# Order of the scatter products in three pairs of experts, the engine of every fifth low part, and the count of filler products

## The chip, the cores and the metric

The kernel runs on one core of one Trainium2 chip, as one launch. The metric is the device time of that core in microseconds. Three runs of the kernel before took 717.22, 717.87 and 718.0 us; their median is 717.87 us. All tensors in memory are float32.

## The reference, cut to what matters

Two layers over 256 tokens of width 1024. Each layer has one combined projection, three kinds of attention heads, an output projection, a LayerNorm, a mixture of 16 experts of which each token takes two, and another LayerNorm.

```python
for layer in range(2):
    y   = h @ w_in[layer]                          # (256,1024) @ (1024,3672), columns split among the heads
    mix = concat(gla(y), moba(y), dsa(y)) @ w_out[layer]
    h   = layer_norm(alpha * h + mix)
    scores = sigmoid(h @ router_w)                 # 16 experts in 4 groups
    # best group by the sum of its two best scores; two experts in it, weights normalised
    ffn = sum_e combine[:, e] * ((silu(h @ w_gate[e]) * (h @ w_up[e])) @ w_down[e])
    h   = layer_norm(alpha * h + ffn)
```

Every expert's three matrices (6 MB each expert) are read from memory in each layer.

## The kernel before, in words

**Two tiles of tokens.** The 256 tokens lie in two tiles of 128 rows, called t = 0 and 1.

**The projections.** `w_in` and `w_out` are taken in 88 pieces for each layer (`weight_pieces`, in the order of `ORDER` and `OUT_ORDER`): 16 pieces of 292 columns, 8 of 512, 16 of 256 and 272 in turn, and 48 of 512. A piece is split into a high part `whi` (ScalarE, a copy that rounds to fp32r) and a low part `wlo` (the difference), in `Pieces.fill`; activations are split likewise into `hhi` and `hlo`. A product of float32 is then three fp32r products: high by high, low activation by high weight, high activation by low weight. Low parts are VectorE's, but of the pieces from number 24 on every fifth (numbers 24, 29, 34, ... 84: 13 in a layer) has its low part from GpSimd (constants `SHARE`, `FROM`). The first two pieces of layer 1 are filled ahead of time, with low parts by GpSimd, through the argument of `pieces.fill(pool)`. The very first block of layer 0 (`project` with `first`) multiplies tile 0 in plain float32 straight from the loaded weights, while pieces are being split.

**The order of the work** in the projections is written by a planner, the class `Order` (lines 77 to 250). Each engine has a clock there; every call adds a cost from `_Lane.cost` (a low part of 512 columns costs 597 ns on VectorE and 1176 ns on GpSimd, a float32 product of 128 columns 215 ns), and tasks such as `indexer`, `decays`, `qk`, `attend`, `linear` and `gated` go on as soon as what they ask for is due by TensorE's clock. Some steps wait until VectorE's planned clock is no more than 300 or 400 ns ahead of TensorE's. After the projections the order is the order of the code.

**Filler products.** `warm(n, w)` (line 562) issues 2n products of 128 columns, of `w` and `ones`, into a bank that nobody reads: 14 at the start of the program, on `ones` (line 759), 4 in the choice of experts (line 1492), 8 between the layers (line 1662). A float32 product shows as two records in the trace.

**The choice of experts.** `choose(t)` (line 1296) is a chain of small VectorE operations for each tile. Its counts are one bf16 product for each tile (line 1320), and `gather_two` (line 1351) collects each expert's tokens by products with a 0/1 matrix `G`.

**The experts** go in eight pairs (loop at line 1563). A pair has a gate product (8 steps, `gate` and `step`), an up product (8 steps), the activations (`av`, SiLU by ScalarE, the product by VectorE), their turn by four transposes on TensorE and a copy on ScalarE (`turn`, line 1583, tiles `aT` and `actT`), and a down product (`y`). A step is two products of 512 columns, one for each expert, on the two halves of the array: four records. The result of a pair, weighted (`by_tile`), is added to the tokens' rows `z` one pair later by `scatter` (line 1418): four fp32r products of 512 columns into four banks (two for each tile of tokens), each followed by an addition on VectorE.

Between a pair's up product and its down product TensorE issues, in pair 0, two steps of the next pair's gate product, the turn, and a third step; in pairs 1, 3 and 5 the gathering of two more pairs with the turn inside it, and then the four scatter products; in pairs 2, 4 and 6 the scatter products of tile 0, in pairs 2 and 4 one step of the next pair's gate product, the turn, the scatter products of tile 1, and in pairs 2 and 4 one more step (`FILL`, `LEAN`; lines 1607 to 1613). The last pair has its own way.

The code around the change in pairs 2, 4 and 6:

```python
                scatter(*late[0], (0,))
                if p < LEAN:
                    gate(p + 1, FILL[0])
                turn()
                scatter(*late.pop(), (1,))
                if p < LEAN:
                    gate(p + 1, FILL[1])
```

**Weights** come through one DMA queue (SyncE's) into 33 buffers of 512 KB and some further ones; a buffer is asked for again when its last reader is done.

Of the kernel before, what the change touches and what calls it, by code (L numbers as in the profile page):

```python
# [9 lines left out]
F32 = mybir.dt.float32  # L10
# [34 lines left out]
N_T4 = 9  # L45
N_SM = 10
N_WS = 4
SHARE = 5
FROM = 24
N_WO = 3  # L50
N_UNITS = ((1, 3), (2, 6))
N_WARM0 = 7
N_AHEAD = 5
LAG = 350.0
TRIG = 5487.999999999999
N_FILL = 2
N_LAST = 2
N_WARM = 2
N_LEAD = 7
N_WARM2 = 4  # L60
TWO = (1, 3, 5)
AGAIN = {(0, 'g', 5), (1, 'g', 2), (1, 'g', 0), (1, 'd', 1), (1, 'd', 6), (1, 'd', 4), (2, 'g', 3), (2, 'd', 6)}
FILL = (1, 2)
LEAN = 5
FILL_0 = (2, 3)
SC_AT = 5
# [177 lines left out]
def trunk_kernel(ctx, tc, x, positions, w_in, gate_up, gate_bias, norm_gain, w_out, ln_mix_g, ln_mix_b,  # L244
# [8 lines left out]
    pe, act, dve, pool = od.pe, od.act, od.dve, od.pool  # L253
# [169 lines left out]
    ident = cp.tile([P, P], F32, name="ident")  # L423
# [77 lines left out]
    def mm(o, a, b, start=True, stop=True):  # L501
        pe.matmul(o, a, b, start=start, stop=stop, skip_group_check=True)
# [59 lines left out]
    def warm(n, w):  # L562

        b_ = bank("warm")
        for i in range(2 * n):
            mm(b_[:, 0:P], w, ones)
        od.free(b_)

# [8 lines left out]
    class Pieces:  # L577
# [8 lines left out]
        def fill(self, eng=dve):  # L586
            while self.i < len(self.plan) and self.i < self.j + self.ahead:
                key, kk, c0, n = self.plan[self.i]
                src = feed[key][:, kk, c0:c0 + n]
                hi = t2("whi", (P, n), F32R)  # L590
                lo = t2("wlo", (P, n), F32R)
                act.activation(hi, src, AF.Copy)
                (pool if self.i % SHARE == SHARE - 1 and self.i >= FROM else eng).tensor_sub(lo, src, hi.bitcast(F32))
                units[key] = feed[key]
                self.made[self.i] = hi, lo
                self.left[key] -= 1
                if not self.left[key]:
                    feed.pop(key)
                    more()
                self.i += 1  # L600
# [165 lines left out]
    for l in range(DEPTH):  # L766
# [529 lines left out]
        def choose(t):  # L1296

            s, g = slice(t * E, t * E + E), slice(4 * t, 4 * t + 4)
            top1, top2 = (top[:, i:i + 1] for i in (2 * t, 2 * t + 1))
            x4 = sel[:, s].rearrange("p (g e) -> p g e", e=4)  # L1300
            xa, xj = (x4[:, :, :, None].to_broadcast([P, 4, 4, 4]), x4[:, :, None, :].to_broadcast([P, 4, 4, 4]))
            rank4 = rank[:, s].rearrange("p (g e) -> p g e", e=4)
            yield dve.tensor_add(sel[:, s], sc[:, s], rb)
            dve.tensor_add(sums[:, g, 0:2], x4[:, :, 0:2], x4[:, :, 2:4])
            dve.tensor_add(sums[:, g, 2:4], x4[:, :, 0::2], x4[:, :, 1::2])
            rev = bass.AP(tensor=sel.tensor, offset=sel.offset + t * E + 3, ap=[sel.ap[0], [4, 4], [-1, 2]])
            yield dve.tensor_add(sums[:, g, 4:6], x4[:, :, 0:2], rev)
            dve.tensor_reduce(gs[:, g], sums[:, g], AX.X, OP.max)
            yield dve.tensor_tensor(gt[:, g], xj, xa, op=OP.is_gt)
            dve.tensor_reduce(top1, gs[:, g], AX.X, OP.max)  # L1310
            yield dve.tensor_tensor(ge[:, g], xj, xa, op=OP.is_ge)
            dve.scalar_tensor_tensor(at[:, g], gs[:, g], top1, pref[:, 0:4], op0=OP.is_equal, op1=OP.mult)
            yield dve.copy_predicated(gt[:, g], below[:, None].to_broadcast([P, 4, 4, 4]), ge[:, g])
            dve.tensor_reduce(top2, at[:, g], AX.X, OP.max)
            yield dve.tensor_reduce(rank4, gt[:, g], AX.X, OP.add)
            yield dve.tensor_scalar(at[:, g], at[:, g], top2, None, op0=OP.is_ge)
            yield dve.scalar_tensor_tensor(hot[:, s].rearrange("p (g e) -> p g e", e=4), rank4, 1.5,
                                           at[:, g, None].to_broadcast([P, 4, 4]), op0=OP.is_lt, op1=OP.mult)
            if t == 0:
                mm(pc[:, 0:E], strict, hot[:, 0:E])  # L1320
            else:
                mm(pc[:, E:2 * E], strict, hot[:, E:2 * E])
            yield dve.tensor_scalar(pos[:, s], hot[:, s], -1000.0, 1000.0, op0=OP.mult, op1=OP.add)
            yield dve.tensor_add(pos[:, s], pos[:, s], pc[:, s])
# [189 lines left out]
        late = []  # L1514
# [40 lines left out]
        def gate(p, upto):  # L1555

            if p not in gates:
                gates[p], done_k[p] = bank("gu"), 0
            while done_k[p] < upto:
                step(p, "g", gates[p], done_k[p])  # L1560
                done_k[p] += 1

        for p in range(E // 2):
            final = p == FIN
            if final:
                Gw = weights(p)
            gate(p, KT)
            av = t2("act")
            act.activation(av, gates[p], AF.Silu)
            if not final:  # L1570
                Gw = weights(p)
            if p in TWO:
                G = t1("G", (P, NT, 4, CAP))
                for t in range(NT):
                    slots(G[:, t], t, 2 * p + 2)
            bu = bank("gu")
            for k in range(KT):
                step(p, "u", bu, k)
            dve.tensor_mul(av, av, bu)
            od.free(gates[p], bu)  # L1580
            sT, ws = by_slot(Gw, final)

            def turn():
                b_ = bank("aT")
                b3 = b_.rearrange("p (a n) -> p a n", a=4)
                for f in range(4):
                    tr(b3[:, f], av[:, f * P:(f + 1) * P])
                aT = t2("actT", (P, 4, P))
                act.activation(aT, b3, AF.Copy)
                od.free(b_)  # L1590
                made.append(aT)

            made = []
            if final:
                for n in range(2):
                    for t in range(NT):
                        begin(t, n)
                turn()
            elif p == 0:
                gate(1, FILL_0[0])  # L1600
                turn()
                gate(1, FILL_0[1])
            elif p in TWO:
                gather_two(p + 1, turn, G)
                scatter(*late.pop())
            else:
                scatter(*late[0], (0,))
                if p < LEAN:
                    gate(p + 1, FILL[0])
                turn()  # L1610
                scatter(*late.pop(), (1,))
                if p < LEAN:
                    gate(p + 1, FILL[1])
            aT, = made
            py = [bank("y") for _ in range(2)]
            yt = [None, None]
            ud = [feed.pop((l, "d", p, i)) for i in range(8)]
            for i in range(8):
                n, k = (i // 4, i % 4) if p >= FIN - 1 else (i % 2, i // 2)
                for e in range(2):  # L1620
                    u = ud[2 * k + e]
                    mm(py[n][64 * e:64 * e + 64], aT[:, k, 64 * e:64 * e + 64], part(u, n), start=k == 0, stop=k == 3)
                    if n:
                        if (p, 2 * k + e) in VECS:
                            vecs.append(lnvec((ln_mix_g, ln_mix_b, ln_ffn_g, ln_ffn_b)[len(vecs)], l))
                        else:
                            used(l, p, "d", 2 * k + e, u)
                if k == 3:
                    yt[n] = [t2("yt", dt=F32R) for _ in range(2)]
                    if final:  # L1630
                        split(py[n], *yt[n], scale=ws)
                    else:
                        by_tile(py[n], yt[n], ws)
                if (p, "d", i) in REST:
                    residual(*divmod(REST.index((p, "d", i)), 2))
                if final:
                    t = i - LAST_AT
                    if t in range(NT):
                        place(sb[t, 0], t, 0, yt, sT, start=False)
                        sts.append(sm("st", 12).rearrange("p (a b) -> p a b", a=2))  # L1640
                        dve.bn_stats(sts[t][:, 0], sb[t, 0])
            od.free(*py)
            late.append((p, yt, sT))
            if p == FIN - 1:
                more(2)
                if l + 1 < DEPTH:
                    mixer_constants(l + 1)
            if p == 0:
                rmax = nc.values_load(cnti[0:1, 0:1], min_val=0, max_val=L)
# [71 lines left out]
```

## Time and profile before

| what | value |
|---|---|
| runs of the kernel before | 717.22, 717.87, 718.0 us, median 717.87 |
| the profiled execution: its own time, its span | 717.56 us, 715.5 us |
| TensorE products busy | 687.1 us, 96% |
| VectorE busy | 443.9 us, 62% |
| ScalarE busy | 273.6 us, 38% |
| GpSimd busy | 75.0 us, 10% |
| read from memory | 242.13 MB, 340 GB/s over the span |
| mean granted TensorE clock | 0.993 |

The span is the time from the first to the last instruction; the profiled execution's own time has 2.06 us around it. The stages of the span: the start to 14.6 us, layer 0's projections and attention to 140 us, the choice of experts to 150 us, its experts to 342 us, the passage to layer 1, its projections from 365 to 490 us, the choice to 505 us, its experts to some 704 us, and the last LayerNorm. In the views times are microseconds from the span's start unless marked ns; PE is TensorE's products, PEld its weight loads, DVE VectorE, ACT ScalarE, POOL GpSimd, SP SyncE. What stands in brackets or behind `<-` at the end of a row is the time that the engine idled just before, and who ended it. All calls go through one helper, so that nearly all instructions have line 239, and are told apart by their tiles.

### The profile page before, as it was taken

To read this page: it belongs to the slowest core of one execution; us is meant where nothing else is said; L and a number is where in the kernel's file an instruction comes from. 1 tells how busy PE (TensorE), PEld (TensorE's weight loads), DVE (VectorE), ACT (ScalarE), POOL (GpSimd) and SP (SyncE) were. 2 spreads that over 40 slices of the span, in tenths; PEclk is the share of its full clock that TensorE was granted. 3 is DMA by queue.
4 is the path that set the end of the run, shared out by engine and by line. 5 is a ranking of instruction groups with operands and counts; after the bars stand their busy time and mean duration, and the time that the engine had idled before them with its cause. 6 is when DMAs were issued, how large, how long until landed. Compare 5 with 4: busy or idle time off the path is not lost. (4 is left out here: it accounts for less than half of the span.)

```text
span 715.5 us, 11300 instructions
## 1 busy us (share of the span) xinstructions
PE 687.1 (96%) x3885; PEld 399.2 (56%) x3885; DVE 443.9 (62%) x1091; ACT 273.6 (38%) x579; POOL 75.0 (10%) x102
## 2 busy tenths in 40 slices
PE   9999999999999989999899999999999999899993
PEld 8887878843533533533487879787435334343330
DVE  6778887652445454767487787867243556259646
ACT  5578675431212201212276676564223022022121
POOL 2021022200000001200121111121000000021002
PEclk9999999999999999999999999999999999999997
DMA  9799937979999999999999844479899999999971
GB/s 306 272 388 407 408 120 250 325 293 408 409 403 408 407 407 408 408 410 407 334 391 401 313 154 146 132 251 338 323 408 408 403 407 409 407 407 409 409 288 59
DMA packets 83533, 244.05 MB, mean 341 GB/s; under 512 B 10180, under 2 KB 14344, under 8 KB 83464
## 3 DMA queue, kind: packets, MB, share of 16 engines
q1 hardware_dynamic: 82792, 242.91, 89.0%
q8 instruction: 34, 0.56, 0.3%
q10 hardware_dynamic: 416, 0.26, 0.1%
q14 instruction: 35, 0.29, 0.1%
q0 software_dynamic: 256, 0.03, 0.0%
HBM read 242.13 MB, written 1.05 MB: 340 GB/s over the span
## 5 line engine op out<-in xcount | busy, mean ns | idle before, releaser
L239 PE MATMUL gu<-wf,xT 128*64 128x512 f32 x912 | 226.0, 594 | 3.6 <-PEq L1437 3.6
L239 DVE SCALAR_TENSOR_TENSOR yt<-y,ws,yt 32x512 fp32r<-32x512 f32 (+1 forms) x116 | 86.7, 748 | 94.9 <-ACT yt L239 93.4
L239 PEld LDWEIGHTS gu<-wf,xT 128*64 128x64 f32 x912 | 71.8, 137 | 131.7 <-issue 123.3
L239 DVE TENSOR_TENSOR wlo<-wf,whi 128x512 fp32r<-128x512 f32 (+3 forms) x148 | 89.6, 640 | 39.5 <-ACT whi L239 28.5
L239 PE MATMUL y<-wf,actT 128*64 128x512 f32 x432 | 110.5, 595 | 1.8 <-ACT actT L239 1.8
L239 ACT ACTIVATE whi<-wf 128x512 fp32r<-128x512 f32 (+3 forms) x176 | 86.1, 553 | 9.8 <-PE po L239 3.6
L239 PE MATMUL pj<-whi,hhi 128*128 128x512 f32 (+2 forms) x224 | 77.4, 356 | 0.4 <-ACT whi L239 0.4
L239 ACT ACTIVATE yt<-y,ws 128x512 fp32r<-128x512 f32 x60 | 36.8, 687 | 104.5 <-PE y L239 94.9
L239 PE MATMUL pj<-whi,hlo 128*128 128x512 f32 (+2 forms) x224 | 75.4, 347 | 0.0
L239 PEld LDWEIGHTS y<-wf,actT 128*64 128x64 f32 x432 | 34.0, 137 | 54.1 <-issue 42.0
L239 DVE TENSOR_TENSOR act<-act,gu 128x512 f32<-128x512 f32 x16 | 11.0, 688 | 83.7 <-PE gu L239 77.1
L239 PE MATMUL pj<-wlo,hhi 128*128 128x512 f32 (+2 forms) x224 | 60.5, 356 | 0.4 <-DVE wlo L239 0.4
L239 POOL TENSOR_TENSOR wlo<-wf,whi 128x512 fp32r<-128x512 f32 (+3 forms) x28 | 32.4, 1158 | 220.1 <-ACT whi L239 183.6
L239 PE MATMUL gu<-wx,xT 128*64 128x512 f32 x112 | 52.7, 596 | 0.0
L239 PEld LDWEIGHTS pj<-whi,hhi 128*128 128x128 f32 x224 | 42.1, 188 | 7.3 <-issue 1.7
L239 PEld LDWEIGHTS pj<-whi,hlo 128*128 128x128 f32 x224 | 42.1, 188 | 4.7
L239 ACT ACTIVATE actT<-aT 128x512 f32<-128x512 f32 x16 | 9.5, 594 | 85.4 <-PE aT L239 85.4
L239 PEld LDWEIGHTS pj<-wlo,hhi 128*128 128x128 f32 x224 | 37.5, 188 | 6.6 <-issue 1.2
L239 ACT ACTIVATE xT<-xT,cols 128x256 f32<-128x256 f32 x32 | 17.4, 564 | 57.2 <-PE xT L239 57.2
L239 ACT ACTIVATE act<-gu 128x512 f32<-128x512 f32 x16 | 9.6, 597 | 75.9 <-PE gu L239 75.9
L239 PE MATMUL y<-wx,actT 128*64 128x512 f32 x80 | 33.4, 595 | 0.0
L239 DVE TENSOR_TENSOR z<-z,sc 128x512 f32<-128x512 f32 x48 | 29.7, 680 | 0.4 <-PE sc L239 0.4
(268 smaller groups left out, 948.1 us busy)
## 6 DMA issues: line engine op xcount, KB each, us to landing
wf<-in_w_expert_gate_dram SPq DMA_DIRECT2D x114, 512.0 KB, 10.2
wf<-in_w_expert_up_dram SPq DMA_DIRECT2D x114, 512.0 KB, 10.1
wf<-in_w_expert_down_dram SPq DMA_DIRECT2D x108, 512.0 KB, 10.0
wf<-in_w_in_dram SPq DMA_DIRECT2D x32, 512.0 KB, 9.8
wx<-in_w_expert_down_dram SPq DMA_DIRECT2D x36, 256.0 KB, 5.9
wf<-in_w_out_dram SPq DMA_DIRECT2D x16, 512.0 KB, 11.1
wx<-in_w_expert_up_dram SPq DMA_DIRECT2D x24, 256.0 KB, 6.9
wx<-in_w_expert_gate_dram SPq DMA_DIRECT2D x10, 512.0 KB, 10.1
```

Of the source, the lines that this page charges most:

```text
L239: return fn(*a, **kw)
```

## The change

The low parts of all pieces go to VectorE, except those of the two pieces filled ahead for layer 1, where GpSimd is still handed in. `warm(n, w)` issues n products instead of 2n; its counts become 11 at the start (14 before), 4 in the choice and 8 between the layers (both as before), and there are 2 new ones on `ident` in `choose(0)`, behind the count's product. In pairs 2, 4 and 6 all four scatter products stand ahead of the turn; in pairs 2 and 4 both steps of the next gate product stand behind it, in pair 6 nothing does.

```diff
-SHARE = 5
-FROM = 24
-N_WARM0 = 7
+N_WARM0 = 11
+N_KEEP = 2
-N_WARM = 2
+N_WARM = 4
-N_WARM2 = 4
+N_WARM2 = 8
-FILL = (1, 2)
+FILL = 2
...
     def warm(n, w):
         b_ = bank("warm")
-        for i in range(2 * n):
+        for i in range(n):
             mm(b_[:, 0:P], w, ones)
         od.free(b_)
...
                 act.activation(hi, src, AF.Copy)
-                (pool if self.i % SHARE == SHARE - 1 and self.i >= FROM else eng).tensor_sub(lo, src, hi.bitcast(F32))
+                eng.tensor_sub(lo, src, hi.bitcast(F32))
...
             if t == 0:
                 mm(pc[:, 0:E], strict, hot[:, 0:E])
+                warm(N_KEEP, ident)
...
             else:
-                scatter(*late[0], (0,))
+                scatter(*late.pop())
+                turn()
                 if p < LEAN:
-                    gate(p + 1, FILL[0])
-                turn()
-                scatter(*late.pop(), (1,))
-                if p < LEAN:
-                    gate(p + 1, FILL[1])
+                    gate(p + 1, FILL)
```

## Rows read from the trace of the kernel before

**Rows 1.** Busy time by stage: length, five engines, granted clock, DMA share, GB/s

```profile
14.60:140.00 125.40, 124.19 (x835) 103.32 (x834) 98.87 (x271) 81.85 (x193) 18.64 (x19) 1.00 0.85 309
...
365.00:490.00 125.00, 122.27 (x821) 101.91 (x820) 97.97 (x263) 80.46 (x189) 21.40 (x20) 1.00 0.70 248
...
505.00:692.00 187.00, 184.93 (x906) 73.12 (x903) 96.62 (x193) 37.15 (x65) 7.32 (x8) 1.00 1.02 402
692.00:704.00 12.00, 10.47 (x45) 3.57 (x43) 2.90 (x4) 1.97 (x3) 0.00 (x0) 1.00 0.04 16
```

**Rows 2.** TensorE's waits: who for whom, us in total, times, longest

```profile
PE y L239 <- ACT actT L239: 1.8, 4, 0.7
```

**Rows 3.** Order of time, TensorE at the start: start, us, engine, line, operation, tiles

```profile
1.05 5.88 PE L239 MATMUL warm<-ones 128*128 128x128 f32 x28 [1.05 <-POOL ones L363]
...
6.43 0.50 PE L239 MATMUL warm<-ones 128*128 128x128 f32 x3
6.76 7.54 PE L239 MATMUL pj<-wf,hT 128*128 128x292 f32 x30
```

**Rows 4.** Order of time, ScalarE at the start

```profile
5.50 0.78 ACT L239 ACTIVATE whi<-wf 128x292 fp32r<-128x292 f32 x2 [2.94 <-DMA wf<-in_w_in_dram]
...
11.32 0.63 ACT L239 ACTIVATE hhi<-hT 128x512 fp32r<-128x512 f32 x1 [1.57 <-DMA hT<-in_x_t_dram]
```

**Rows 5.** Groups of instructions: busy us, mean ns, idle before

```profile
L239 DVE TENSOR_TENSOR wlo<-wf,whi 128x512 fp32r<-128x512 f32 x94 | 67.2, 740 | 30.8 <-ACT whi L239 19.9 <-issue 7.5 <-PE po L239 2.4
...
L239 DVE TENSOR_TENSOR y<-rope 128x128 f32<-128x128 f32 x8 | 3.4, 420 | 0.4
```

**Rows 6.** Order of time, layer 0 from 67.9 us

```profile
67.97 0.68 DVE L239 TENSOR_TENSOR wlo<-wf,whi 128x512 fp32r<-128x512 f32 x1
...
68.97 1.28 POOL L239 TENSOR_TENSOR wlo<-wf,whi 128x512 fp32r<-128x512 f32 x1 [6.45 <-ACT whi L239]
69.09 1.31 DVE L239 TENSOR_TENSOR y<-rope 128x128 f32<-128x128 f32 x1
...
70.46 0.66 PE L239 MATMUL tr<-ident,y 128*128 128x128 f32 x4 [0.75 <-DVE y L239]
```

**Rows 7.** Order of time, layer 1 from 413.9 us

```profile
413.94 2.38 DVE L239 TENSOR_TENSOR wlo<-wf,whi 128x512 fp32r<-128x512 f32 x2
...
414.15 1.63 POOL L239 TENSOR_TENSOR wlo<-wf,whi 128x512 fp32r<-128x512 f32 x1 [6.07 <-ACT whi L239]
...
417.07 0.68 PE L239 MATMUL bT<-mc,la 128*128 128x128 f32 x4 [0.59 <-DVE la L239]
```

**Rows 8.** Order of time, TensorE in pair 2 of layer 0

```profile
213.48 0.71 PE L239 MATMUL sc<-yt,sT 128*128 128x512 f32 x2
...
216.66 0.59 PE L239 MATMUL gu<-wf,xT 128*64 128x512 f32 x1
217.09 0.60 PE L239 MATMUL y<-wx,actT 128*64 128x512 f32 x2
```

**Rows 9.** Order of time, TensorE in pairs 0 and 1 of layer 0

```profile
167.42 0.66 PE L239 MATMUL aT<-ident,act 128*128 128x128 f32 x4
...
168.91 0.60 PE L239 MATMUL y<-wf,actT 128*64 128x512 f32 x2
...
191.44 1.17 PE L239 MATMUL sc<-yt,sT 128*128 128x512 f32 x4
192.54 0.64 PE L239 MATMUL y<-wf,actT 128*64 128x512 f32 x1
```

**Rows 10.** Order of time, TensorE in pair 6 of layer 0

```profile
313.58 0.71 PE L239 MATMUL sc<-yt,sT 128*128 128x512 f32 x2
314.34 0.66 PE L239 MATMUL aT<-ident,act 128*128 128x128 f32 x4
...
315.68 0.65 PE L239 MATMUL y<-wf,actT 128*64 128x512 f32 x2 [0.22 <-ACT actT L239]
```

**Rows 11.** Order of time, TensorE in the choice of experts, layer 0

```profile
147.24 0.94 PE L239 MATMUL xT<-G,h 128*128 128x128 f32 x6 [1.08 <-DVE top L239]
```

## The prediction

> **What bounds the kernel now.** I read the busy time by stage first, since the change touches three kinds of stage. The reader is to see that TensorE is busy for 124.2 of 125.4 us in layer 0's projections, 122.3 of 125.0 in layer 1's, and 184.9 of 187.0 in layer 1's experts, while VectorE has some 27 us free in each projection stage [rows 1]. So time comes out only where TensorE itself has less to do, or where one of its few waits goes. The list of TensorE's waits comes next: among experts the wait for the turned activations is 1.8 us in four places [rows 2]; the order of time then tells whose they are. Last come the order of time at the start, at two waits in the projections, and in pairs 2 and 6, record by record, because the price of a reordered product can be read only there.
>
> The sum below is made against the profiled execution's own 717.56 us (its span and 2.06 us around it); that lies 0.31 us below the runs' median of 717.87, and I give the forecast at the median's height.
>
> **The start: 14 filler products become 11.** The first 25 of the 28 records take 5.38 us (1.05 to 6.43), 0.215 us each; the last three take 0.11 us each up to 6.76, where the projection begins without a gap [rows 3]. That is TensorE at 1.2 and then at 2.4 GHz. Twenty-two records at 0.215 us end at 5.78 us, 0.98 us earlier. The data allow that: ScalarE starts on the first weights at 5.50 us [rows 4]. From 5.78 to about 6.2 the projection's records run at the lower level and lose half of 0.4 us, so it is 0.77 us ahead. It doesn't stay so. The first pass is 8 blocks of four records of 0.246 us (30 in 7.4 us, [rows 3]), and its seventh block begins at 6.76 + 24 x 0.246 = 12.66 us. The last tile of activations lands at 11.32 us, where ScalarE's wait for it ends [rows 4], and the seventh weight tile, 292 KB, is next in the queue: at some 400 GB/s [rows 1] it lands at 12.05. That block can start at about 12.1 us, 0.57 us ahead. I take **-0.57 us**; ends 0 (the clock rises later, below) and -0.98. What is late next is the landing of that tile.
>
> **Two filler products behind the count.** Four records of 0.11 us [rows 3], 0.44 us a layer, stand where TensorE idles 1.08 us for VectorE's chain of choosing [rows 11]. The product behind them waits for `G` in any case, so the idle time hides them: **0**; without it +0.9 us for two layers. They can't give anything back: the granted clock is 1.00 in all the stages around [rows 1]. The counts 4 and 8 are the numbers of products there were.
>
> **Low parts by VectorE.** GpSimd loses 26 of its 28, 13 in each layer: 18 of 512 columns and 8 of about half that. On VectorE they cost at most 18 x 0.74 + 8 x 0.37 = 16.3 us [rows 5], 8.2 us a layer, on stages where it has 27 us free: its share goes from 79% to 85%. Up to four pieces are made ahead (three in the output projection), so this free time has to fail over several pieces before a product is late. Against it stands what GpSimd's work costs VectorE now. At 68.97 us a low part starts on GpSimd and takes 1.28 us; the small addition of `qk` that starts 0.12 us later ends 0.15 us after it, having taken 1.31 us [rows 6]. The other seven of its kind average (8 x 0.42 - 1.31) / 7 = 0.29 us [rows 5]. TensorE idles 0.75 us for exactly this result [rows 6]. Without GpSimd's instruction the addition ends at 69.4 us, before TensorE asks for it at 70.46 - 0.75 = 69.71; the low part itself comes behind the next low part in VectorE's order, so behind the addition. I count -0.70 us. In layer 1 two of VectorE's low parts take 2.38 us from 413.94 beside GpSimd's 1.63 us, 1.0 us more than two undisturbed ones (2 x 0.68, [rows 6]), and TensorE idles 0.59 us for `la`, which comes next on VectorE [rows 7]. There the moved low part may stand ahead of `la` (1.0 - 0.68 [rows 6], so 0.3 us gained) or behind it (all 0.59): -0.45 us. The other 24 I cost at nothing: they add 0.4 to 0.7 us each and take away as much where they held something. Together **-1.15 us**; ends -2.5 (as much again at places that I can't see) and +4 (a quarter of the 16.3 us reaches TensorE).
>
> **Pairs 2 and 4.** The stretch from the first scatter product to the down product takes 217.09 - 213.48 = 3.61 us [rows 8]. The new order is made of pieces seen elsewhere. Four scatter products in a row and what follows: 192.54 - 191.44 = 1.10 us. Turn and a first gate step behind it: 168.91 - 167.42 = 1.49 us [rows 9]. A further step: twice the 0.43 us of two records, 0.86 us [rows 8]. Sum 3.45, so 0.16 us less; TensorE loses something at each change of the kind of product, and there are two fewer. Nothing waits anew: the turn begins at 213.48 + 1.10 = 214.6 us, 1.10 us behind the first scatter product, and in pair 6 it starts 0.76 us behind it [rows 10], so the activations are there. From the turn to the down product pair 6 needs 1.34 us for ScalarE's copy [rows 10]; here the turn and the two steps behind it take 2.35, which covers it. The four banks are freed by the same additions in the same order; VectorE's, ScalarE's and the weight queue's orders don't change. Four such pairs in two layers: **-0.64 us**; ends 0 and -0.8.
>
> **Pair 6.** The diff takes its cover away, though it has no gate step: now scatter products of tile 1 stand between the turn and the down product, which still idles 0.22 us for ScalarE's copy [rows 10]. From the turn's start to the down product it is 315.68 - 314.34 = 1.34 us, a chain that doesn't get shorter. The new turn starts at 313.58 + 1.10 = 314.68 us, so the down product at 316.02, 0.34 us later. Two layers: **+0.68 us**, all on the path; ends +0.4 and +1.2.
>
> **Sum.** -0.57 - 1.15 - 0.64 + 0.68 = -1.68 us: 715.9 us beside the profiled execution, **716.2 us** beside the median. The planner sees three filler products less and 26 dearer calls on VectorE's clock, so tasks may take other places in the projections. That has no row; by the two waits above, one misplaced wait is worth 0.6 to 0.75 us, so I put 1 us on either side: 715.2 to 717.2.
>
> **Rivals.**
> *Half comes out, nothing can be told.* The new places of tasks make a wait like the two that go. For it: TensorE's idle time in these stages is 1.2 and 2.7 us [rows 1], in single waits of 0.4 to 0.7 us. Against it: these two had a plain cause that is taken away. Without the low parts' gain: 717.87 - 0.53 = 717.3 us.
> *VectorE becomes the bound in the projections* (slower). From the point where a low part is done later than the last product of its high part ends, each further one delays TensorE by 0.7 us. If an eighth to a quarter of the 16.3 us gets through: +2 to +4 us, 719.4 to 721.4. For it: VectorE is nearly full in places, and GpSimd's low parts ran ahead of their need. Against it: 85% on average.
> *The clock rises later at the start* (slower). The 32 records of the first pass would then take up to 0.25 us more each. Even half of them late is +3.9 us, 721. Against it: TensorE goes from filler to projection without a gap, as before.
> *More is held than I see.* VectorE's low parts average 0.74 us where an undisturbed one takes 0.68, 94 of them [rows 5, 6]: 5 us of holding, some 4 of it beside the place in layer 1, spread thin. If a quarter of that is on TensorE's path, 715.2 us. The Trainium skill (SBUF — State Buffer, Who interferes with whom) says that a VectorE instruction with two inputs in SBUF and a GpSimd instruction that reads SBUF exclude each other for the whole length of the one that came first. The row at 69.09 us agrees (1.31 us, ended with GpSimd's); by that rule alone all 26 places could give something back.
> *The weight stream decides the end.* It runs at 402 GB/s to 692 us and is all but silent after [rows 1], while TensorE still works to 704. Time gained ahead of layer 1's experts moves the stream too; only the 0.3 us gained within them could be lost.
>
> **How the numbers follow.** A measurement of this kernel can tell about 0.2%, 1.44 us, so below 716.43 is faster. Forecast 48% (two thirds of it beyond that line), half 25%, VectorE the bound 10%, late clock 5%, more held 12%. Faster 0.48 x 2/3 + 0.12, about 0.44; slower 0.15; the rest, 0.41, within. The range reaches from 714.6 to 718.8 us.
>
> **What would show it.** Right: the projection's first record near 5.8 us; no wait of the transposes at 69 us on `y`; no VectorE addition of 1.3 us; down products of pairs 2 and 4 3.45 us behind their first scatter product; pair 6's wait for `actT` 0.65 us or so. Wrong: waits of `pj` for `wlo` above 1 us; a first pass at 0.49 us a record; new waits in the projections.

## The result, and the profile after

The changed kernel takes 723.83 us (median of 6 runs, 723.39 to 724.2), the kernel before 717.91 us beside it (6 runs). The ratio is 1.0078, 95% interval [1.0063, 1.0093]: slower by 5.9 us, where 716.2 us was forecast. The profiled execution took 724.01 us, with a span of 722.3 us; it lies 6.45 us above the profiled execution of before, and their spans differ by 6.8 us.

**Where the time went.** The table gives the start of some products, in us from the span's start, as the two traces have them, and what each stage between two of them gained or lost (from the unrounded starts).

| first product of | before | after | the stage that ends there |
|---|---|---|---|
| layer 0, on split weights (`whi`) | 14.42 | 14.19 | -0.23 |
| layer 0, experts (`gu`) | 151.30 | 155.97 | **+4.91** |
| layer 0, down products of pair 2, 4, 6 (`y`) | 217.09, 268.15, 315.68 | 221.47, 272.29, 320.03 | -0.30, -0.23, +0.20 |
| layer 1, on split weights | 365.22 | 369.58 | about 0 |
| layer 1, experts | 503.47 | 510.73 | **+2.90** |
| layer 1, down products of pair 2, 4, 6 | 569.26, 620.32, 667.86 | 576.23, 626.95, 674.67 | -0.30, -0.34, +0.19 |
| the span's end | 715.48 | 722.29 | about 0 |

The sum is 6.8 us, the whole difference of the spans. The experts gained 0.78 us in all, where the forecast had them about even (-0.64 and +0.68 us); both losses lie in the projections. The busy time by stage says the same (after; stretch, length, then PE, PEld, DVE, ACT, POOL with their counts, granted clock, DMA share, GB/s; the first three answer to [rows 1]):

```profile
14.60:144.67 130.07, 127.17 (x834) 105.92 (x833) 98.54 (x284) 82.79 (x194) 4.28 (x6) 0.97 0.81 296
369.36:497.26 127.90, 123.83 (x821) 102.66 (x820) 98.34 (x276) 82.06 (x190) 5.37 (x7) 0.99 0.68 244
512.26:698.81 186.55, 184.10 (x906) 73.88 (x903) 96.56 (x193) 37.15 (x65) 7.32 (x8) 1.00 1.02 402
55.00:58.40 3.40, 3.40 (x16) 2.69 (x15) 2.62 (x9) 3.36 (x6) 0.00 (x0) 0.50 1.03 411
123.20:126.60 3.40, 3.40 (x26) 3.05 (x26) 2.18 (x6) 1.19 (x2) 1.01 (x1) 0.50 0.49 154
478.20:481.60 3.40, 3.40 (x28) 3.01 (x29) 2.18 (x6) 1.19 (x2) 1.01 (x1) 0.50 0.44 153
```

Two things are to be seen. VectorE did 13 low parts more in layer 0 (284 instructions for 271) and was busy no longer: 98.54 us for 98.87. So VectorE did not become the bound by its load. And TensorE's clock, 1.00 in all these stages before, fell to 0.50 of full speed (1.2 GHz) in three short stretches. TensorE's waits, after (who for whom, us in total, times, longest; the third line answers to [rows 2]):

```profile
PE pT L238 <- DVE s_sb L238: 4.2, 2, 2.1
...
PE y L238 <- ACT actT L238: 2.7, 4, 0.7
...
PE xT L238 <- DVE top L238: 1.1, 2, 0.5
```

The first line is new: twice 2.1 us, once in each layer, for the softmax (`s_sb`) of the second tile of the selected attention (the one whose keys the indexer selects). The waits for `y` and `la` [rows 6, 7] are gone. In the order of time on TensorE (after; start, us, engine, line, operation, tiles) this wait stands in the middle of the output projection `po`, and the middle one of the half-speed stretches begins right behind it:

```profile
120.02 0.62 PE L238 MATMUL po<-whi,mx 128*128 128x512 f32 x2
120.48 0.39 PE L238 MATMUL po<-wlo,mx 128*128 128x512 f32 x1
122.96 1.17 PE L238 MATMUL pT<-ident,s_sb 128*128 128x128 f32 x5 [2.10 <-DVE s_sb L238]
```

In the kernel before (same view) the transposes `pT` and their products `pv` came at 111 us, ahead of the whole output projection, and without a wait:

```profile
110.92 1.03 PE L239 MATMUL pT<-ident,s_sb 128*128 128x128 f32 x8
111.89 1.58 PE L239 MATMUL pv<-pT,v 128*64 128x128 f32 x24
```

VectorE's order of time shows what the transposes waited for (after):

```profile
116.93 0.41 DVE L238 CUSTOM_DVE_ANT_0 s_sb<-sc,acc 128x256 f32<-128x256 f32 x1
...
118.42 0.17 DVE L238 TENSOR_SCALAR mx<-mx 128x4 f32<-128x4 f32 x1
118.50 0.69 DVE L238 TENSOR_TENSOR wlo<-wf,whi 128x512 fp32r<-128x512 f32 x1
121.74 0.69 DVE L238 TENSOR_TENSOR wlo<-wf,whi 128x512 fp32r<-128x512 f32 x1 [2.54 <-ACT whi L238]
122.34 0.17 DVE L238 RECIPROCAL ri<-mx 128x4 f32<-128x4 f32 x1
122.55 0.88 DVE L238 TENSOR_SCALAR s_sb<-s_sb,ri 128x256 f32<-128x256 f32 x3
```

From the scores to the scaled softmax it is 6.0 us (116.93 to 122.96), a chain over VectorE, ScalarE (four exponentials, then a high part) and VectorE again. What the written order puts beside it on TensorE, some products `o` of another head and a part of the output projection, ends at 120.86 us. Not all of the 6.0 us is the softmax's own. Its last exponential is done at 120.71 us, as ScalarE's order of time shows (after), but its reciprocal `ri` stands in VectorE's order behind a low part, and that one waits for the high part:

```profile
120.52 0.19 ACT L238 ACTIVATION_READ_ACCUMULATOR s_sb<-s_sb,mx 128x1 f32 x1
...
121.09 0.62 ACT L238 ACTIVATE whi<-wf 128x512 fp32r<-128x512 f32 x1
```

The records of the output projection, of this attend's `pT` and `pv`, and of the transposes of `og`, each counted to the start of the next record, come to 25.30 us in layer 0 before and 30.09 after (+4.79), in layer 1 to 25.57 and 30.08 (+4.51). That covers the loss of layer 0, and more than that of layer 1, where other waits went (-1.61, of it 0.59 that for `la`). In layer 0 two more things work against each other: in the first of the half-speed stretches thirteen projection products take 4.00 us from the first start to the last (from 55.90 us), where the same ones take 2.87 in a run below with this order and the clock at 1.00, and the 0.75 us wait for `y` is gone.

### The profile page after: what moved, and what is told of

Its sections match the earlier page's. It is cut to its first block, busy times and chain, and to the rows that moved or that the text cites. A ratio compares the mean times of both kernels' runs of the same rounds, so it can differ in the third digit from the quotient of the medians.

```text
span 722.3 us, 11300 instructions
## 1 busy us (share of the span) xinstructions
PE 691.1 (96%) x3887; PEld 404.8 (56%) x3887; DVE 443.7 (61%) x1117; ACT 276.1 (38%) x581; POOL 44.6 (6%) x76
## 5 line engine op out<-in xcount | busy, mean ns | idle before, releaser
L238 DVE TENSOR_TENSOR wlo<-wf,whi 128x512 fp32r<-128x512 f32 (+3 forms) x174 | 97.2, 598 | 55.8 <-ACT whi L238 52.4
L238 DVE TENSOR_SCALAR xT<-xT,cols 128x256 f32<-128x256 f32 x32 | 16.9, 543 | 13.6 <-ACT xT L238 13.2
```

The source lines that it names most:

```text
L238: return fn(*a, **kw)
```

## The experiments

**Why the attend is late: two theories.** The planner now puts every fifth low part on VectorE's clock, and the selection of the indexer goes on only while that clock is at most 400 ns ahead of TensorE's. Theory 1: the planner's order costs the time. Rival: VectorE's added work does. Four kernels, run together (before: 717.97 us), part the two.

*The engine alone*: the kernel before; VectorE executes every fifth low part, but the planner is charged for GpSimd, so the order stays.

```diff
+                fifth = self.i % SHARE == SHARE - 1 and self.i >= FROM
+                if fifth:
+                    h32 = hi.bitcast(F32)
+                    od.note("POOL", pool.cost("tensor_sub", lo, [src, h32], {}), [src, h32], [lo])
+                    nc.vector.tensor_sub(lo, src, h32)
...
```

> The kernel before with one change: the 26 low parts run on VectorE, while the planner is still charged as if GpSimd ran them, so that every engine's written order stays that of before. Theory 1, the planner's new order costs the time: no wait of pT for s_sb of 2 us, no half clock inside, and the two waits at 69 and 416 us gone: about 1 us faster than before, 716.4 to 717.4. Rival, VectorE's added load costs it: some 5 us slower, 722 to 724, with TensorE waiting for wlo or s_sb.

719.12 us, ratio 1.0011 [1.0, 1.0022]. No loss of 6 us, and not the gain of 1.15 either. The waits for `y` at 69 us and for `la` are gone as forecast, and others have come, among them 0.78 us for a softmax at 80 us. VectorE's order of time in this kernel shows why (line 597 is the moved low part):

```profile
78.94 0.69 DVE L597 TENSOR_TENSOR wlo<-wf,whi 128x512 fp32r<-128x512 f32 x1 [1.41 <-ACT whi L239]
...
80.67 0.28 DVE L239 MATCH_REPLACE8 acc<-m,acc 128x128 f32<-128x128 f32 x1
80.86 0.17 DVE L239 RECIPROCAL ri<-mx 128x4 f32<-128x4 f32 x1
81.06 0.88 DVE L239 TENSOR_SCALAR s_sb<-s_sb,ri 128x128 f32<-128x128 f32 x4
```

The moved low part waits 1.41 us for its high part, and all that is queued behind it on VectorE waits with it; on GpSimd that wait held up nobody. In layer 1 the same happens at 430.73 us (0.71 us for `whi`), and TensorE pays there:

```profile
434.29 0.28 PE L239 MATMUL gq<-hhi,wlo 128*128 128x256 f32 x1
435.63 0.41 PE L239 MATMUL tr<-ident,y 128*128 128x128 f32 x2 [1.07 <-DVE y L239]
```

From the first product on split weights to the experts, this kernel takes 0.10 us more than before in layer 0 and 0.79 us more in layer 1.

*The order alone*: the opposite. GpSimd executes, the planner is charged for VectorE.

```diff
...
+                    od.note("DVE", dve.cost("tensor_sub", lo, [src, h32], {}), [src, h32], [lo])
+                    nc.gpsimd.tensor_sub(lo, src, h32)
...
```

> The kernel before with the other half: GpSimd still runs the 26 low parts, but the planner is charged as if VectorE ran them, so that TensorE's order in the projections is that of the changed kernel. Theory 1: both waits of 2 us for s_sb come back and the clock falls behind them, 722 to 725. Rival, VectorE's load: VectorE has no more to do than before, so no change, 717 to 719.

727.45 us, ratio 1.0134 [1.0111, 1.0157]: the loss without any added work on VectorE, and 3.6 us more than the changed kernel, above the range that was expected. Its waits on TensorE hold the new line and two more for VectorE:

```profile
PE pT L239 <- DVE s_sb L239: 4.2, 2, 2.1
...
PE tr L239 <- DVE og L239: 2.7, 2, 1.4
...
PE tr L239 <- DVE y L239: 1.5, 2, 0.8
```

The waits for `y` are of its own (0.63 us in layer 0, 0.85 in layer 1), and in its profile the choice of experts of layer 1 took 1.53 us more than before, at a clock of 0.51 from 508.4 us. The waits for `og` come up again below. One half of its expectation missed: the clock did not fall behind the two waits of 2.10 us. Order of time on TensorE, then the stretch in the view by windows, both of this kernel:

```profile
122.94 1.23 PE L239 MATMUL pT<-ident,s_sb 128*128 128x128 f32 x8 [2.10 <-DVE s_sb L239]
...
127.03 1.23 PE L239 MATMUL tr<-ident,og 128*128 128x128 f32 x8 [1.35 <-DVE og L239]
```

```profile
120.00:126.60 6.60, 3.58 (x36) 2.52 (x34) 3.69 (x10) 3.37 (x9) 1.01 (x1) 1.00 0.25 79
```

*The low parts alone*: the kernel before with this one edit of the change.

```diff
-                (pool if self.i % SHARE == SHARE - 1 and self.i >= FROM else eng).tensor_sub(lo, src, hi.bitcast(F32))
+                eng.tensor_sub(lo, src, hi.bitcast(F32))
```

> The kernel before with the low parts' edit alone (engine and planner both). Theory 1 and its rival both put the loss here: 723 to 725, as the changed kernel and a little more, since the saving of the other edits (0.5 us) is missing. If the loss sits in the fillers or the pairs: 717 to 718.

723.94 us, ratio 1.0078 [1.0064, 1.0093]. The whole loss comes from this edit.

*All but the low parts*: the changed kernel with that edit undone.

> The changed kernel with every fifth low part given back to GpSimd, so all other edits alone. Theory 1 and its rival: the loss is gone; start, pairs 2 and 4 and pair 6 leave 0.3 to 0.7 us, 717.2 to 717.7. If the loss sits in the fillers or the pairs: 722 or more.

716.55 us, ratio 0.998 [0.9971, 0.9989]. The rest of the change gains 1.4 us, more than the 0.3 to 0.7 that the expectation had. Theory 1 stands; the rival falls as the cause of the 6 us, though VectorE's added work is not free (0.10 and 0.79 us above).

**Clock or wait?** In the changed kernel the clock falls behind the wait; does the fall cost anything? The changed kernel with eight filler products in the wait, not charged to the planner:

```diff
+N_HOLD = 8
...
+                if v0 == 256 and (t, h0) == (1, 0):
+                    for _ in range(N_HOLD):
+                        nc.tensor.matmul(b_[:, 0:P], ident, ones, start=True, stop=True, skip_group_check=True)
```

> The changed kernel with eight filler products (128 columns, results not used, not charged to the planner) ahead of the first transposes of the second tile of the selected attend, where TensorE waits 2.1 us for the softmax in each layer. Theory 1 (the planner's order makes the wait, and the granted clock falls behind it because TensorE stands): the wait itself stays, as it is VectorE's to end, but the clock no longer falls at 123 and 478 us; a stretch at half clock costs about 1.5 us, so 720.8 us, 3 us less than the changed kernel's 723.8. Rival (the half clock has another cause, or costs nothing since other waits shrink beside it): 723.8 us, with the stretches at 123 and 478 us still at half clock.

723.12 us, ratio 1.0076 [1.0063, 1.0089]: no 3 us. The granted clock is 1.00 in both stretches, but a new wait takes the place of the slow records. Order of time on TensorE in this kernel (the first row has half of the fillers' records):

```profile
119.75 1.06 PE L649 MATMUL pT<-ones,ident 128*128 128x128 f32 x8
121.13 1.23 PE L239 MATMUL pT<-ident,s_sb 128*128 128x128 f32 x8 [0.33 <-DVE s_sb L239]
122.29 1.58 PE L239 MATMUL pv<-pT,v 128*64 128x128 f32 x24
125.29 0.41 PE L239 MATMUL tr<-ident,og 128*128 128x128 f32 x2 [1.42 <-DVE og L239]
```

The records summed above, with the fillers, come to 29.81 us here for 30.09 with the slow clock (layer 1: 29.79 for 30.08). The transposes of `og` begin 4.16 us behind the first `pT` (121.13 to 125.29), and in the changed kernel, at half speed and without a wait, just as late (122.96 to 127.12). In the run with the order alone, at full speed and without fillers, it is 4.09 us, with the wait of 1.35 us for `og`. The chain over VectorE sets the end; a slower TensorE only arrived later at the next wait. The half clock behind this wait cost 0.3 us a layer, not the 1.5 I had put on it.

**Can the order be mended?** The bound of the selection raised from 400 to 1000 ns, in the changed kernel:

```diff
-                    yield lambda: od.clk["DVE"] <= od.clk["PE"] + 400
+                    yield lambda: od.clk["DVE"] <= od.clk["PE"] + 1000
```

> The changed kernel with one number of the planner changed: the selection of the indexer may go on while VectorE's planned clock is up to 1000 ns (instead of 400) ahead of TensorE's. The order that is written then has the selected attend finished ahead of the output projection again. Theory 1 (VectorE, charged with the low parts, looks late to the planner, which then defers the selection, and the selected attend comes behind the start of the output projection): the two waits of 2.1 us for the softmax and the half clock behind them go, 2 x 3.6 = 7.2 us of 723.8, and 716.6 us are left. Rival (VectorE's added work itself is what is late): the softmax waits move to another place and it stays within 1 us of 723.8.

721.28 us, ratio 1.0057 [1.0042, 1.0072], between the two theories. The softmax waits are gone, as theory 1 says. But the order of the first of the two selections and of the decays changed as well, and TensorE waits for three results of the decays; from 53.2 to 60 us its granted clock is 0.50, and again from 408.2 to 411.5 us. Order of time on TensorE in this kernel:

```profile
49.24 0.39 PE L238 MATMUL tr<-ident,rank 128*16 128x128 f32 x2 [0.46 <-ACT W L238]
...
51.03 0.50 PE L238 MATMUL pj<-whi,hhi 128*128 128x512 f32 x1 [0.90 <-ACT W L238]
...
54.14 0.80 PE L238 MATMUL rw<-mc,ones 128*128 128x128 f32 x2 [1.26 <-DVE mc L238]
```

So the bound was raised for the second selection only:

```diff
-                    yield lambda: od.clk["DVE"] <= od.clk["PE"] + 400
+                    yield lambda: od.clk["DVE"] <= od.clk["PE"] + (400 if t else 2500)
```

> The changed kernel with the planner's bound raised for the second of the two selections of the indexer alone (VectorE's planned clock may be 2500 ns instead of 400 ahead of TensorE's; the first selection keeps 400, so that the order ahead of it stays that of the changed kernel). The selected attend is then written ahead of the output projection. Theory 1 (the deferred selection is what costs the time; the waits at 48 to 53 us of the run with one bound of 1000 came from the first selection): the stretch from the softmax to the output projection loses its 4.7 us in layer 0 and 4.3 us in layer 1, 723.8 - 9.0 = 714.8 us. Rival (VectorE, with 26 low parts more, is late wherever the attend stands): other waits for VectorE of together 4 us or more come up, over 719 us.

716.24 us, ratio 0.9975 [0.9963, 0.9987]. One number of the planner gives back 7.6 us: the changed kernel, with all low parts on VectorE, is then faster than the kernel before. Order of time on TensorE in this kernel, the attend ahead of the output projection again:

```profile
110.74 1.03 PE L238 MATMUL pT<-ident,s_sb 128*128 128x128 f32 x8
111.71 1.14 PE L238 MATMUL pv<-pT,v 128*64 128x128 f32 x16
113.06 0.66 PE L238 MATMUL pv<-pT,v 128*64 128x128 f32 x8 [0.21 <-ACT pT L238]
...
116.50 0.63 PE L238 MATMUL po<-whi,mx 128*128 128x512 f32 x2
```

My 714.8 us was too low. By the sums above 4.8 and 4.5 us could at most have come back, and not all did: the records summed above come to 25.97 us in each layer, not to the 25.30 and 25.57 of before, with small waits like the one shown, and the first product on split weights came 0.39 us later than in the changed kernel's profile.

The other way to the old order is to charge the planner for GpSimd in the changed kernel, as in the first experiment:

> The whole change, with the low parts executed by VectorE, but the planner charged for every fifth of them as a GpSimd operation, so that the order is that of the kernel before around them. Theory 1 (the new order makes all of the loss): no softmax wait, no half clock behind it; from the run without the low parts, 716.55 us, and the +0.75 us that the trace of the run with the engine alone showed: 717.3 us. The prediction's own term for the low parts (-1.15) would give 715.4 us. Rival (the load on VectorE makes the loss together with the other parts of the change): over 720 us.

717.04 us, ratio 0.9985 [0.9974, 0.9996], as theory 1 said. All of the change in the old order loses nothing; against the run without the low parts (716.55 us) they cost about 0.5 us, which the two intervals don't part; in its trace the projections take 0.12 and 0.80 us more than before, as with the engine alone.

**The small parts.** The start alone, in the kernel before:

```diff
-N_WARM0 = 7
+N_WARM0 = 11
```

(with n products for 2n in `warm`, and the other two counts doubled).

> The kernel before with the start's filler products alone in the changed form (products on ones instead of twice as many on the identity, in the changed counts); the order of everything else is that of before. Theory 1 (the end of the filler products sets the first projection's start, and everything behind it moves up): 717.35 us, 0.57 less than before's 717.9. Rival (the weights' transfers set the layer's pace a few us later, so the gain is lost there): 717.9 us.

718.76 us, ratio 1.0012 [1.0003, 1.0021]: a miss. The profile has the gain, 0.50 us at the first product on split weights, and holds it to the choice of experts. There the transposes of the tokens behind the 1.08 us wait for `top` [rows 11] ran at the lower clock and took 1.4 us longer. Order of time on TensorE, then the stretch in the view by windows, both of this kernel:

```profile
146.76 2.05 PE L239 MATMUL xT<-G,h 128*128 128x128 f32 x8 [1.08 <-DVE top L239]
```

```profile
146.70:150.10 3.40, 3.34 (x17) 3.31 (x18) 1.60 (x10) 0.01 (x1) 0.00 (x0) 0.55 1.04 399
```

The profile of before has this stretch at 1.00, and eight such records take 1.18 us there. So the two filler products at the count might do more than fill idle time. They alone, in the kernel before:

```diff
+N_KEEP = 1
...
                 mm(pc[:, 0:E], strict, hot[:, 0:E])
+                warm(N_KEEP, ident)
```

> The kernel before with two filler products behind the routing's first position product in each layer, and nothing else. Its runs so far fall in two groups, 717.1 to 717.8 and 718.0 to 719.0 us, and one profile of the kernel with the start alone changed showed the token transposes behind that wait at half clock, 1.3 us longer. Theory (the filler products keep the clock up there): all runs in the lower group, median about 717.4 us, none from 718.5 up. Rival (the two groups have another cause): two groups as before, median 717.6 to 718.0 us.

717.69 us, ratio 0.9989 [0.9978, 1.0001]; runs of 717.13 to 718.18 us, and before's beside them of 717.0 to 721.05, with 13 of 35 above 718.5. The interval includes 1, and the medians differ by 0.2 us. But the other runs lean the same way. In the order of before, a mean granted clock of 0.991 or less came up in 43 of 103 executions without these fillers (28 of 81 of the kernel before, 6 of 11 with the engine alone, 9 of 11 with the start alone) and in 1 of 46 with them (this run, all but the low parts, the same with pair 6 in its old order, and the change in the old order). Some of these kernels differ in other edits too, and with the raised bound 9 of 24 executions show the lower clock in spite of the fillers. So it is likely, not shown, that the fillers give something back; the means of this run and of before's beside it, 717.68 and 718.23 us, lie 0.55 us apart.

Pair 6 back in its old order, first without the low parts, then with the raised bound:

```diff
-                scatter(*late.pop())
-                turn()
                 if p < LEAN:
+                    scatter(*late.pop())
+                    turn()
                     gate(p + 1, FILL)
+                else:
+                    scatter(*late[0], (0,))
+                    turn()
+                    scatter(*late.pop(), (1,))
```

> The run that had all of the change but the low parts, with pair 6 in its old order again (half of the scatter products ahead of the activations' turn, half behind), pairs 2 and 4 in the new one. Theory 1 (the pairs' terms add up: -0.28 for each of pairs 2 and 4, +0.19 for each pair 6): 0.38 us less than that run's 716.55, so 716.2 us. Rival (pair 6's wait is paid back in the stage that follows): 716.55 us.

> The changed kernel with the second selection's bound at 2500 ns and pair 6 of the experts in its old order. Theory 1: 2 x 0.19 us less than the run with the bound alone, 714.4 us. Rival (the pair's 0.19 us is paid back in the next stage): the same as that run.

716.49 us, 0.9981 [0.9972, 0.9989], and 716.47 us, 0.9971 [0.9958, 0.9985]: neither can be told from its partner (716.55 and 716.24 us). In both traces pair 6 has its old length again, so the 0.19 us each is real there; in the second profile the last 24 down products took 6.09 us instead of 5.37 and ate it. Why they did was not found.

## Why the prediction was wrong, step by step

**The step that failed** is the last one of the sum: that the planner sees dearer calls on VectorE's clock and "tasks may take other places in the projections", priced by the two waits of before at 0.6 to 0.75 us, with "1 us on either side". Measured, one task in another place cost 4.8 and 4.5 us in the records summed above (layers 0 and 1). The size could have been bounded from what I had written down myself: 9 low parts of 512 columns and 4 of about half that, at 597 ns and half of it, put some 6.6 us a layer on a clock that may lead TensorE's by no more than 400 ns where the selection is to go on. A task held back so can slide by microseconds until it stands in front of a stage with too little else to do. The price is then the chain behind it (scores to softmax 6.0 us) less the work that TensorE has left to lay beside it, and not the size of the waits that happen to stand in the trace of before. That gives the first wait, 2.1 us; what stands behind the softmax in VectorE's order comes late with it, which is the wait of 1.35 to 1.42 us for `og` in the two runs at full clock. The remaining 1.0 to 1.3 us were not traced to single waits. I took the planner's change for noise around the sum; it was the largest term.

**Low parts, -1.15 us.** Right: both waits went, and what held VectorE went. The low parts of 512 columns fell from 740 ns each [rows 5] to 686, the small additions from 420 to 292. Groups of instructions on VectorE after (busy us, mean ns, idle before):

```profile
L238 DVE TENSOR_TENSOR wlo<-wf,whi 128x512 fp32r<-128x512 f32 x112 | 73.6, 686 | 45.7 <-ACT whi L238 44.2 <-PE po L238 1.3
...
L238 DVE TENSOR_TENSOR y<-rope 128x128 f32<-128x128 f32 x8 | 2.3, 292 | 0.3
```

The Trainium skill (SBUF — State Buffer, Who interferes with whom) says that a VectorE instruction with two inputs in SBUF and a GpSimd instruction that reads SBUF exclude each other at the shared port. The traces agree, for with GpSimd's low parts gone VectorE did 13 more a layer within nearly the same busy time (98.54 us for 98.87, and 98.34 for 97.97). Wrong: that this time reaches TensorE. In the old order the term measured +0.9 us in the trace (0.10 and 0.79), not -1.15, since a low part on VectorE stands in a queue. I had asked whether VectorE has time for them, not what is queued behind one that waits for its high part; "the other 24 I cost at nothing" is where that was passed over.

**The rivals.** "Half comes out" named the right mechanism, new places of tasks, at a price six times too small. "VectorE becomes the bound" named the right sign for a wrong reason: its busy share stayed, and no product waited longer for `wlo`. The late clock at the start came in small: three records of the first pass were slow, where one or two were forecast. "More is held than I see" was right of VectorE and worth nothing, as VectorE was not on the path there.

**Pairs 2 and 4, -0.64 us.** The mechanism was right, the size too small: -0.30, -0.23, -0.30, -0.34, together -1.17. Pair 2, after (answers to [rows 8]):

```profile
218.16 1.18 PE L238 MATMUL sc<-yt,sT 128*128 128x512 f32 x4
219.17 0.60 PE L238 MATMUL aT<-ident,act 128*128 128x128 f32 x4
...
221.47 1.03 PE L238 MATMUL y<-wx,actT 128*64 128x512 f32 x4
```

The four scatter products take 1.01 us up to the turn. I had put 1.10, the time up to a down product [rows 9]: the change of kind there costs 0.09 us more than the one to a transpose. The rest, 2.30 us, had been put at 2.35.

**Pair 6, +0.68 us.** The wait came as said, 0.69 us, and the loss was +0.39 for both layers: 1.01 + 1.29 = 2.30 us from scatter to down product, for 2.10 before, where I had added 1.10 + 1.34. Pair 6, after (answers to [rows 10]):

```profile
317.73 1.18 PE L238 MATMUL sc<-yt,sT 128*128 128x512 f32 x4
318.74 0.60 PE L238 MATMUL aT<-ident,act 128*128 128x128 f32 x4
320.03 1.51 PE L238 MATMUL y<-wf,actT 128*64 128x512 f32 x6 [0.69 <-ACT actT L238]
```

**The start, -0.57 us.** The projection begins at 5.91 us, 0.13 us behind where the arithmetic put it (order of time on TensorE, after; answers to [rows 3]):

```profile
1.05 5.06 PE L238 MATMUL warm<-ones 128*128 128x128 f32 x22 [1.05 <-POOL ones L362]
5.91 1.53 PE L238 MATMUL pj<-wf,hT 128*128 128x292 f32 x3
```

Of the 0.86 us there, 0.23 us are left at the first product on split weights, since the first three records of the projection take 1.37 us from start to start (5.905 to 7.275), where 0.74 would do. In the eight other profiles with this start, what is left there lies between 0.57 us gained and 0.16 us lost. The five profiles with the old start differ among themselves as much (14.01 to 14.61 us); the means of the two groups, 14.06 and 14.37 us, lie 0.31 us apart. The term is right in kind, and about half as large as forecast. The limit that I had named, the landing of the seventh weight tile, shows as a wait in none of them. Where the projection begins earlier than here, its fifth record waits for the landing of the second weight tile instead: 0.33 us with all but the low parts (begun at 5.44 us), 0.79 us with the raised bound (begun at 5.59 us).

**The filler at the count, 0.** They lie in the idle time as said: the wait for `top` is 0.5 us for 1.1. That they could give nothing back rested on a clock of 1.00 in one profile; the run with the start alone shows that the same place can run at 0.55, 1.4 us slower.

With the order restored, the change with the raised bound takes 716.24 us, where 716.2 was forecast. That is luck and not the forecast coming true: in it the low parts stand at +0.5 us or so where I had -1.15, and the pairs gave more.

## What to carry to other kernels

Where an order is made by a planner with clocks, moving work from one engine to another moves every task that is held back by that clock: build the order's new position of the long chains into the sum, and price a displaced chain by its own length less the work left to cover it, and add what stands behind it in the same queue; don't price it by the waits that exist. An instruction moved onto a busy in-order engine brings its own wait with it: ask what stands behind it in the queue, before asking whether the engine has free time. A filler that restores the clock in front of a chain on another engine buys little (0.3 of 1.5 us here), for TensorE only reaches the next wait sooner.

## What the runs showed of the hardware that was not expected

TensorE's granted clock fell to half behind single waits of 2.1 us (those that ended at 122.96 and 477.74 us in the changed kernel), around one of 1.08 us (ended at 146.76 us, with the start alone), and in the changed kernel at 55.0 us, where the two waits just before were of 0.39 and 0.40 us. None of these waits brings it about by itself. The two of 2.10 us in the run with the order alone, the 1.08 us in the kernel before, and 0.38 and 0.40 us at the place of the third in the run with fillers in the wait left the clock at 1.00. One profile with the clock at 1.00 in a place doesn't show that it is safe there. And 26 low parts more on VectorE (16 us by their durations) hardly changed its busy time in the projections, in the run with the engine alone too (98.18 and 98.11 us, for 98.87 and 97.97 before): GpSimd's competing instructions had cost it about as much.
